# How the masked decays of the second attention are put together in DRAM: accumulating transfers, or plain copies with a skewed write of the mask

## The chip, the cores and the metric

One core of one Trainium2 chip runs the whole program in one launch. The metric is the device time of that launch in microseconds (us). For the kernel before, three timed runs gave 971.83, 976.06 and 982.13 us, so the median is 976.06.

## The reference

The program is a two-layer decoder trunk on 256 tokens of width 1024, all in float32. Layer one holds a differential attention, layer two a "forgetting" attention; each attention sits between two SwiGLU feed-forward blocks, with RMS norms and shifts, scales and gates from a conditioning vector. What the change touches is the logits of the second attention, with 16 heads of width 64:

```python
log_f = jax.nn.log_sigmoid((h @ fgate_w + fgate_b))
F = jnp.cumsum(log_f, axis=1)                     # (b, 256, 16)
...
decay = F[q] - F[k]                               # per head
logits = q @ k.T * scale + decay
logits = jnp.where(q_pos >= k_pos, logits, -inf)
p = softmax(logits)
```

The term F[q] is the same for a whole row, so the softmax does not see it; the kernel adds only -F[k], scaled by 8 because the scores are scaled by 1/8 afterwards, and a large negative constant (-1e30) above the diagonal.

## The kernel before, in words

Every large product is done in three passes: a weight arrives as float32 (`raw`, six buffers of 128 x 1024), ScalarE (ACT) casts its high part (`wh`, six buffers), VectorE (DVE) subtracts to get the low part (`wl`, five buffers), and TensorE (PE) multiplies high by high, low by high and high by low. A tile of such a weight is called a piece here. SyncE (SP) issues the loads of `raw` and of `ada`, the 1 MB blocks of conditioning weights that DVE multiplies and sums in its spare time (the custom operation `ada<-ada,cact,vecs`). The order on PE, ACT, DVE and SP is written out by the program itself (class `InOrder`, L54 to L100, keeps a clock per engine and fills gaps with casts and subtractions; L99 is the one line that records every such instruction). GpSimd (POOL) is called directly as `nc.gpsimd`; its instructions are put in order by the scheduler of the tile framework, and its DMAs go through the software queue q0. The loads by SP go through q1. Both queues use the same 16 DMA engines.

The second attention needs, for each head, a 128 x 384 tile `d` of decays: columns 0 to 127 belong to the first block of 128 queries (keys 0 to 127), columns 128 to 383 to the second block (keys 0 to 255). Each of the two has one 128 x 128 diagonal block, in which the upper triangle must carry the constant.

* While the last value projection of the shared keys and values runs (L1196 to L1228), `fk` (16 heads x 256, minus 8 F[k]) is made at step 7 (L1206 to L1211). POOL stores it twice in DRAM as `fdram`, 384 numbers a head (L1214, L1215). Sixteen DMAs (L1219) then copy each head's 384 numbers to 128 rows of `dmask`, and sixteen more (L1222) add the 128 x 128 mask, which lies in SBUF in the tile `tri`, to the two diagonal blocks of each head: an accumulating DMA, `accum_op=ALU.add`.
* Then a feed-forward block runs, `ffn(1, 0, ...)` (L1232): eleven pairs `pg`, `pu`, and eight outputs `po`. It needs none of this.
* `attention_b` (L1234) begins with two query projections `lp` (`late_pairs`, L1255) while `decay(c)` (L1248) loads the tiles `d0` to `d9` from `dmask`, two for each pair of heads `c`. Their buffers are shared with the hidden tiles of the feed-forward block (tags `hidh2` to `hidh7`, `hidl6` to `hidl9`, list `DT`), so a load waits for the last reader of its buffer. For each pair, `scores` makes the products `sb`, `exps` (L1272) adds the decay with the row minimum on DVE and takes the exponential on ACT, `scale` (L1286) divides, and `weights_t` (L1296) transposes the six 128 x 128 blocks on PE; `values` multiplies by the values. Four projections `lq` and the steps of the output projection `pw` fill PE between these groups.

Of the kernel before, what the change touches and what calls it, by code (L numbers as in the profile page):

```python
# [10 lines left out]
F32 = mybir.dt.float32  # L11
F32R = mybir.dt.float32r
BF16 = mybir.dt.bfloat16
AF = mybir.ActivationFunctionType
ALU = mybir.AluOpType
PSUM = bass.MemoryType.PSUM

P = 128
D = 1024
S = 256  # L20
# [3 lines left out]
BH = 16  # L24
# [5 lines left out]
BIG = 3.0e38  # L30
# [13 lines left out]
NRAW = 6  # L44
NLO = 5
NHI = 6

V_NORM = 0
V_KVN = 48
# [54 lines left out]
def trunk(ctx, tc, a, out):  # L104
    nc = tc.nc
    InOrder.ready = {}
    pe = InOrder(tc, nc.tensor, 0.0, 1 / 2350)
    act = InOrder(tc, nc.scalar, 0.13, 1 / 1200)
    dve = InOrder(tc, nc.vector, 0.08, 1 / 960)
# [14 lines left out]
    def abank(name):  # L124
        return pp.tile([P, 512], F32, tag="ta", name=name)
# [786 lines left out]
    for k in range(0, NC, 2):  # L912
# [3 lines left out]
        if k % 4:  # L916
            i = k // 4
# [14 lines left out]
    def constants():  # L932
# [44 lines left out]
    ident, mask, ub, skew, nlam, subg = (  # L977
        late[n] for n in ("ident", "mask", "ub", "skew", "nlam", "subg"))
# [217 lines left out]
    for i, (kk, n) in enumerate(v_proj("wkv", vb)):  # L1196
        if mh:
            mh.go()
        run_laters()
        if i == 5:  # L1200
            plf = abank("plf")
            for t in range(2):
                pe.transpose(plf[:, t * BH:(t + 1) * BH], lf[:, t * P:(t + 1) * P], ident[:BH, :BH])
            lft = kp.tile([P, 2 * BH], F32, tag="lft", name="lft", bufs=1)
            act.copy(lft, plf[:, :2 * BH])
        if i == 7:  # L1206
            pFk = abank("pFk")
            mm(pFk[:BH, P:S], lft[:, BH:], ub[:, :P], start=True, stop=False, skip_group_check=True)
            mm(pFk[:BH, :S], lft[:, :BH], ub, start=False, stop=True, skip_group_check=True)
            fk = kp.tile([BH, S], F32, tag="w512b", name="fk")  # L1210
            act.activation(fk, pFk[:BH, :S], AF.Copy, scale=-1.0)  # L1211

            fdram = tc.dram_tile([BH, P + S], F32, name="fdram")
            nc.gpsimd.dma_start(fdram[:, :P], fk[:, :P])  # L1214
            nc.gpsimd.dma_start(fdram[:, P:], fk)  # L1215
            dmask = tc.dram_tile([BH, P, 384], F32, name="dmask")
            m2 = mask.rearrange("p (o k) -> p o k", o=1).to_broadcast([P, 2, P])
            for hd in range(BH):
                nc.gpsimd.dma_start(dmask[hd], bass.AP(fdram.tensor, fdram.offset + hd * (P + S), [[0, P], [1, P + S]]))  # L1219
            for hd in range(BH):  # L1220
                diag = dmask[hd].rearrange("p (b k) -> p b k", k=P)[:, ::2]
                nc.gpsimd.dma_start(diag, m2, accum_op=ALU.add)  # L1222
        if i == 8:
            need(*nm_)
            table(AF.Silu)
            mh = MakeH(rstd, nm_)
            mh.go()
# [6 lines left out]
    def attention_b():  # L1234
        o = {}

        def o_tiles(j):
            h = cp_.tile([P, 512], F32R, tag=f"hidh{j}", name=f"obh{j}")
            l = cp_.tile([P, 512], F32R, tag=f"hidl{4 + j}", name=f"obl{j}")
            for i in range(2):  # L1240
                o[2 * j + i] = h[:, i * 256:i * 256 + 256], l[:, i * 256:i * 256 + 256]

        q = [cp_.tile([P, 512], F32, tag=f"hidl{j}", name=f"q{j}") for j in range(4)]
        ds, sms = {}, {}

        DT = ["hidh4", "hidh5", "hidh6", "hidh7", "hidl8", "hidl9", "hidh2", "hidh3", "hidl6", "hidl7"]

        def decay(c):  # L1248

            for hd in (2 * c, 2 * c + 1):  # L1250
                d = cp_.tile([P, 384], F32, tag=DT[hd % 10], name=f"d{hd}")
                nc.gpsimd.dma_start(d, dmask[hd])
                ds[hd] = d

        r = late_pairs("wq", q[:2], None, AF.Exp)  # L1255
        for c in range(5):
            decay(c)
        op = OutProj(o)
        st = {}
        mode[0] = "fill"  # L1260
        NP = BH // 2

        def scores(c, sb):

            cb = (c % 2) * 256
            for qt, (c0, w) in enumerate(QT):
                for m in range(2):
                    rows = slice(m * HD, m * HD + HD)
                    mm(sb[m][:, c0:c0 + w], q[c // 2][rows, cb + qt * P:cb + qt * P + P],
                       kT[c // 2][rows, cb:cb + w], start=True, stop=True)  # L1270

        def exps(c, sb):  # L1272
            nm = kp.tile([P, 4], F32, tag="nm", name=f"nmb{c}")
            sm = kp.tile([P, 4], F32, tag="smb", name=f"smb{c}", bufs=3)
            for m in range(2):
                d = ds[2 * c + m]
                for qt, (c0, w) in enumerate(QT):
                    cc = 2 * qt + m
                    dve.tensor_tensor_reduce(
                        d[:, c0:c0 + w], sb[m][:, c0:c0 + w], d[:, c0:c0 + w], -0.125, BIG,  # L1280
                        ALU.add, ALU.min, accum_out=nm[:, cc:cc + 1])
                    act.activation(d[:, c0:c0 + w], d[:, c0:c0 + w], AF.Exp,
                                   bias=nm[:, cc:cc + 1], scale=-1.0, accum_out=sm[:, cc:cc + 1])
            sms[c] = sm

        def scale(c):  # L1286

            rs = kp.tile([P, 4], F32, tag="rs", name=f"rsb{c}")
            dve.reciprocal(rs, sms[c])
            for m in range(2):  # L1290
                d = ds[2 * c + m]
                for qt, (c0, w) in enumerate(QT):
                    dve.tensor_scalar(d[:, c0:c0 + w], d[:, c0:c0 + w], rs[:, 2 * qt + m:2 * qt + m + 1], None,
                                      op0=ALU.mult)

        def weights_t(c, ta, tb):  # L1296
            for m, b, to, i in ((0, 0, ta, 0), (0, 1, ta, 1), (0, 2, ta, 2), (1, 2, ta, 3), (1, 0, tb, 0), (1, 1, tb, 1)):
                pe.transpose(to[:, i * P:i * P + P], ds[2 * c + m][:, b * P:b * P + P], ident)

        def weights_out(c, ta, tb):  # L1300
            w0 = cp_.tile([P, 512], F32, tag="hidh8", name=f"wta{c}")
            w1 = cp_.tile([P, 256], F32, tag="hidh9", name=f"wtb{c}")
            act.copy(w0, ta)
            dve.tensor_copy(w1, tb[:, :256])
            st[c] = ((w0[:, :2 * P], w0[:, 2 * P:3 * P]), (w1, w0[:, 3 * P:]))

        def values(c, po):

            for kt in range(2):
                for m in range(2):  # L1310
                    hd = 2 * c + m
                    v = vb[kt][hd // 8][:, (hd % 8) * HD:(hd % 8) * HD + HD]
                    mm(po[m * HD:m * HD + HD, kt * P:], v, st[c][m][kt], start=kt == 0, stop=kt == 1)

        def out_split(c, po):
            if c % 2 == 0:
                o_tiles(c // 2)
            oh, ol = o[c]
            act.copy(oh, po)
            dve.tensor_tensor(ol, po, oh.bitcast(F32), op=ALU.subtract)  # L1320

        def group(t):

            cs, cw, cv = (c if 0 <= c < NP else None for c in (t, t - 1, t - 2))
            sb = [sbank(f"sb{t}_{m}") for m in range(2)] if cs is not None else None
            ta = abank(f"wa{t}") if cw is not None else None
            tb = bbank(f"wb{t}") if cw is not None or cv is not None else None
            if cs is not None:
                scores(cs, sb)
            if cv is not None:  # L1330
                values(cv, tb[:, 256:])
            if cw is not None:
                weights_t(cw, ta, tb)
            if cs is not None:
                plain(exps, cs, sb)
            if cw is not None:
                weights_out(cw, ta, tb)
            if cv is not None:
                out_split(cv, tb[:, 256:])
            if cw is not None and t + 4 < NP:  # L1340
                decay(t + 4)

        def fills():
            for j in (2, 3):
                for _ in late_pair("wq", q[j], r, f"lq{j}"):
                    yield
                    yield
            for _ in range(6):
                for _ in op.steps():
                    yield  # L1350

        fill = fills()
        for t, n in enumerate((3, 9, 7, 7, 8, 8, 7, 7, 7, 5)):
            for i in range(n):
                if 1 <= t <= NP and i == n - 2:
                    scale(t - 1)
                next(fill)
            group(t)
        for _ in range(4):
            next(fill)  # L1360
        return op, fill
# [135 lines left out]
```

## Time and profile before

| what | value |
|---|---|
| timed runs | 971.83, 976.06, 982.13 us |
| the profiled execution, its own time | 971.96 us |
| its span in the trace | 970.1 us |
| granted TensorE clock | 0.998 |
| busy: PE, PE weight load, DVE, ACT, POOL | 959.5, 933.0, 819.2, 551.0, 81.8 us |
| DMA queue q1 (SP's loads) | 259.69 MB |
| DMA queue q0 (POOL's transfers) | 12.16 MB |

The profiled execution is one run, 1.86 us longer than its span, and 4.1 us below the median of the timed ones. Matmuls overlap one another in the pipeline: a matmul of 128 x 256 shows 276 ns, and six of them take 0.68 us on the chain of waits. In the rows of a view, "a<-b" names the tile written and the tiles read, and "DMA landing" is the time from the issue of a transfer to its last byte. The queue rows give packets, megabytes and the time that their packets took as a share of 16 DMA engines over the window asked for.

### The profile page before, as it was taken

The numbers are of one execution on the slowest core, as the hardware profiler recorded it, in microseconds if no ns is written. First come the engines' busy times: TensorE is split into PE (matmuls) and PEld (weight loads), VectorE is DVE, ScalarE is ACT, GpSimd is POOL, SyncE is SP. The second block draws the span as 40 slices with busy tenths as digits, with TensorE's granted clock in tenths as the row PEclk, the third lists the DMA queues.
The fourth block names the chain that finished last, engine by engine and source line by source line (L and its number), as shares of the span: only waits on it lengthen the run. The fifth ranks groups of instructions, "written<-read, shape, count | busy, mean of one in ns | idle before, by whom it ended". The sixth has DMA issues, their size and how long they took to land.

```text
span 970.1 us, 20433 instructions
## 1 busy us (share of the span) xinstructions
PE 959.5 (99%) x8076; PEld 933.0 (96%) x8076; DVE 819.2 (84%) x1372; ACT 551.0 (57%) x894; POOL 81.8 (8%) x126
## 2 busy tenths in 40 slices
PE   8999999999999999999999999999999999999997
PEld 7999999998999999999998999999998899999997
DVE  7989979889999999888889988899978799555575
ACT  5466545566787745545577544545567776555432
POOL 0000200000112000000000720000021014300000
PEclk9999999999999999999999999999999999999999
DMA  9998899967867699888959999998884337987641
GB/s 359 414 359 277 324 377 343 338 227 266 309 202 257 199 373 379 315 267 317 329 190 373 343 357 359 399 369 326 321 321 161 109 110 232 269 156 268 188 150 44
DMA packets 74849, 273.46 MB, mean 282 GB/s; under 512 B 9929, under 2 KB 14833, under 8 KB 64642
## 3 DMA queue, kind: packets, MB, share of 16 engines
q1 hardware_dynamic: 66016, 259.69, 75.3%
q0 software_dynamic: 8448, 12.16, 5.0%
q8 instruction: 63, 1.03, 0.4%
q10 hardware_dynamic: 290, 0.32, 0.1%
q14 instruction: 32, 0.26, 0.1%
HBM read 267.90 MB, written 7.90 MB: 284 GB/s over the span
## 4 chain that ended last, share of the span: by engine, by line
PE 96%; DVE 2%; DMA 1%; ACT 1%; issue 0%; SPq 0%; ACTq 0%; DVEq 0%
PE po L99 25%; PE pg L99 21%; PE pu L99 21%; PE pf L99 5%; PE pv L99 5%; PE pw L99 4%; PE lp L99 4%; PE pqk L99 3%; PE lq L99 1%; PE lg L99 1%; PE lu L99 1%; PE pk L99 1%; DVE ada L99 1%; DMA ada<-in_ada 1%; PE sb L99 1%; PE s L99 1%
## 5 line engine op out<-in xcount | busy, mean ns | idle before, releaser
L99 ACT CAST wh<-raw 128x1024 fp32r<-128x1024 f32 (+1 forms) x360 | 347.2, 975 | 222.8 <-PE po L99 68.2
L99 DVE TENSOR_TENSOR wl<-raw,wh 128x1024 fp32r<-128x1024 f32 (+1 forms) x360 | 398.2, 1125 | 69.3 <-ACT sg L99 17.6
L99 DVE CUSTOM_DVE_ANT_0 ada<-ada,cact,vecs 128x1024 f32<-128x1024 f32 x160 | 203.4, 1278 | 0.4 <-DMA ada<-in_ada 0.4
L99 PE MATMUL pg<-HH,wl 128*128 128x256 f32 x608 | 168.2, 277 | 0.4 <-DVE wl L99 0.4
L99 PE MATMUL pg<-HH,wh 128*128 128x256 f32 x608 | 168.0, 276 | 0.0
L99 PE MATMUL pg<-HL,wh 128*128 128x256 f32 x608 | 167.9, 276 | 0.0
L99 PE MATMUL pu<-HH,wh 128*128 128x256 f32 x608 | 167.9, 276 | 0.0
L99 PE MATMUL pu<-HL,wh 128*128 128x256 f32 x608 | 167.9, 276 | 0.0
L99 PE MATMUL pu<-HH,wl 128*128 128x256 f32 x608 | 167.9, 276 | 0.0
L99 PE MATMUL po<-hidh,wh 128*128 128x256 f32 x528 | 145.7, 276 | 0.0
L99 PE MATMUL po<-hidh,wl 128*128 128x256 f32 x528 | 145.7, 276 | 0.0
L99 PE MATMUL po<-hidl,wh 128*128 128x256 f32 x528 | 145.7, 276 | 0.0
L99 PEld LDWEIGHTS pg<-HH,wl 128*128 128x128 f32 x608 | 114.2, 188 | 0.9 <-DVE wl L99 0.8
L99 PEld LDWEIGHTS pg<-HH,wh 128*128 128x128 f32 x608 | 114.1, 188 | 0.7 <-ACT tri L99 0.6
L99 PEld LDWEIGHTS pg<-HL,wh 128*128 128x128 f32 x608 | 114.2, 188 | 0.0
L99 PEld LDWEIGHTS pu<-HH,wh 128*128 128x128 f32 x608 | 114.2, 188 | 0.0
L99 PEld LDWEIGHTS pu<-HH,wl 128*128 128x128 f32 x608 | 114.2, 188 | 0.0
L99 PEld LDWEIGHTS pu<-HL,wh 128*128 128x128 f32 x608 | 114.1, 188 | 0.0
L99 PEld LDWEIGHTS po<-hidh,wl 128*128 128x128 f32 x528 | 99.1, 188 | 0.0
L99 PEld LDWEIGHTS po<-hidh,wh 128*128 128x128 f32 x528 | 99.1, 188 | 0.0
L99 PEld LDWEIGHTS po<-hidl,wh 128*128 128x128 f32 x528 | 99.1, 188 | 0.0
L99 DVE TENSOR_TENSOR hidl<-hf,hidh 128x512 fp32r<-128x512 f32 x44 | 30.3, 689 | 21.7 <-ACT hidh L99 21.7
(225 smaller groups left out, 1860.9 us busy)
## 6 DMA issues: line engine op xcount, KB each, us to landing
raw<-in_win SPq DMA_DIRECT2D x176, 512.0 KB, 7.7
ada<-in_ada SPq DMA_DIRECT2D x79, 1024.0 KB, 7.7
raw<-in_wout SPq DMA_DIRECT2D x48, 384.0 KB, 5.7
raw<-in_wout SPq DMA_DIRECT2D x48, 320.0 KB, 5.4
raw<-in_wqk SPq DMA_DIRECT2D x16, 512.0 KB, 5.6
raw<-in_wo SPq DMA_DIRECT2D x16, 512.0 KB, 5.5
raw<-in_wlast SPq DMA_DIRECT2D x16, 512.0 KB, 4.3
raw<-in_wv SPq DMA_DIRECT2D x8, 512.0 KB, 6.5
```

The costliest lines, as they stand in the source:

```text
L99: return self.tc.keep_in_program_order(f(*args, **kw))
```

## The change

`fdram` holds each head once (256 numbers). The DRAM tensor is now called `masked` and has 512 columns a row (`DW`) instead of 384. For each of its two parts, columns 0 to 255 (the second query block) and then columns 256 to 383 (the first), four DMAs of four heads each copy `fdram` to all rows, and four DMAs of four heads each write the constant over the upper triangle. The triangle is written as 127 runs of 127 numbers (508 bytes) with a pitch of 513: each run begins one column further right than the one before. What a run writes beyond its block falls into the columns of the next part, which is copied afterwards, or into columns that nobody reads. The source of the runs is one row of the mask in the input `in_misc`, read again and again. In `d` the two parts have changed places, so `exps`, `scale` and `weights_t` address them through `DQ`; every instruction keeps its shape and its turn.

```diff
-            fdram = tc.dram_tile([BH, P + S], F32, name="fdram")
-            nc.gpsimd.dma_start(fdram[:, :P], fk[:, :P])
-            nc.gpsimd.dma_start(fdram[:, P:], fk)
-            dmask = tc.dram_tile([BH, P, 384], F32, name="dmask")
-            m2 = mask.rearrange("p (o k) -> p o k", o=1).to_broadcast([P, 2, P])
-            for hd in range(BH):
-                nc.gpsimd.dma_start(dmask[hd], bass.AP(fdram.tensor, fdram.offset + hd * (P + S), [[0, P], [1, P + S]]))
-            for hd in range(BH):
-                diag = dmask[hd].rearrange("p (b k) -> p b k", k=P)[:, ::2]
-                nc.gpsimd.dma_start(diag, m2, accum_op=ALU.add)
+            fdram = tc.dram_tile([BH, S], F32, name="fdram")
+            nc.gpsimd.dma_start(fdram, fk)
+            masked = tc.dram_tile([BH, P, DW], F32, name="masked")
+            for c0, w in ((0, S), (S, P)):
+                for hd in range(0, BH, 4):
+                    nc.gpsimd.dma_start(masked[hd:hd + 4, :, c0:c0 + w],
+                                        bass.AP(fdram.tensor, fdram.offset + hd * S, [[S, 4], [0, P], [1, w]]))
+                for hd in range(0, BH, 4):
+                    above = bass.AP(masked.tensor, masked.offset + hd * P * DW + c0 + w - P + 1,
+                                    [[P * DW, 4], [DW + 1, P - 1], [1, P - 1]])
+                    nc.gpsimd.dma_start(above, bass.AP(a["misc"].tensor, a["misc"].offset + 2 * P + 1,
+                                                       [[0, 4], [0, P - 1], [1, P - 1]]))
...
+        DQ = (S, 0)
...
-                nc.gpsimd.dma_start(d, dmask[hd])
+                nc.gpsimd.dma_start(d, masked[hd, :, :384])
...
+                    dq = d[:, DQ[qt]:DQ[qt] + w]
                     dve.tensor_tensor_reduce(
-                        d[:, c0:c0 + w], sb[m][:, c0:c0 + w], d[:, c0:c0 + w], -0.125, BIG,
+                        dq, sb[m][:, c0:c0 + w], dq, -0.125, BIG,
                         ALU.add, ALU.min, accum_out=nm[:, cc:cc + 1])
...
-            for m, b, to, i in ((0, 0, ta, 0), (0, 1, ta, 1), (0, 2, ta, 2), (1, 2, ta, 3), (1, 0, tb, 0), (1, 1, tb, 1)):
+            for m, b, to, i in ((0, 2, ta, 0), (0, 0, ta, 1), (0, 1, ta, 2), (1, 1, ta, 3), (1, 2, tb, 0), (1, 0, tb, 1)):
```

On PE, DVE, ACT and SP the list of instructions is the same before and after, in the same order and shapes (7858, 1268, 674 and 261 rows). Only POOL's list differs, in two places. The first is the building of the decays in DRAM, during the value projection and the feed-forward block after it. Before (`fg` is a small weight loaded ahead of it, `x16` means sixteen of the same kind in a row):

```order
L1165 DMA fg<-in_fgw 128x128
L1214 DMA fdram<-fk 16x128
L1215 DMA fdram<-fk 16x256
L1219 DMA dmask<-fdram 128x384 x16
L1222 DMA dmask<-tri 128x2x128 x16
L1252 DMA d_9428<-dmask 128x384
```

Now, with the semaphores that each transfer waits for (DMASW0 to DMASW7 are completion semaphores of POOL's transfers, used in turn):

```order
L1216 DMA fdram<-fk 16x256 [waits Activation_49]
L1220 DMA masked<-fdram 512x1x256 [waits DMASW2_49]
L1220 DMA masked<-fdram 512x1x256 x3
L1225 DMA masked<-in_misc 4x127x127 [waits DMASW7_49,DMASW3_49]
...
L1225 DMA masked<-in_misc 4x127x127 [waits DMASW6_49]
L1220 DMA masked<-fdram 512x1x128 [waits DMASW7_49]
...
L1220 DMA masked<-fdram 512x1x128 [waits DMASW2_49]
L1225 DMA masked<-in_misc 4x127x127 [waits DMASW3_49]
...
L1225 DMA masked<-in_misc 4x127x127 [waits DMASW6_49]
```

Thirty-four transfers have become seventeen, in four steps of four: within a group of four heads, copy, constant, copy and constant each wait for the one before to land, and the four groups overlap.

The second place is the loading of the first ten tiles `d0` to `d9` on POOL, at the end of the feed-forward block. Before:

```order
L1252 DMA d6_9428<-dmask_6811 128x384 [waits DMASW4_49,DVE_49,PE_49]
L1252 DMA d7_9430<-dmask_6811 128x384 [waits DMASW5_49,DVE_49,PE_49]
L1252 DMA d0_9416<-dmask_6811 128x384 [waits DMASW6_49,DVE_49,PE_49]
L1252 DMA d1_9418<-dmask_6811 128x384 [waits DMASW7_49,PE_49]
L1252 DMA d2_9420<-dmask_6811 128x384 [waits DMASW0_49,DVE_49,PE_49]
L1252 DMA d8_9432<-dmask_6811 128x384 [waits DMASW1_49,PE_49]
...
L1252 DMA d5_9426<-dmask_6811 128x384 [waits DMASW4_49,DVE_49,PE_49]
L1252 DMA d9_9434<-dmask_6811 128x384 [waits DMASW5_49]
```

Now:

```order
L1258 DMA d0_9399<-masked_6810 128x384 [waits DMASW7_49,DVE_49,PE_49]
L1258 DMA d1_9401<-masked_6810 128x384 [waits PE_49]
L1258 DMA d2_9403<-masked_6810 128x384 [waits DVE_49,PE_49]
L1258 DMA d3_9405<-masked_6810 128x384 [waits DVE_49,PE_49]
L1258 DMA d4_9407<-masked_6810 128x384 [waits DMASW0_49,DVE_49,PE_49]
L1258 DMA d5_9409<-masked_6810 128x384 [waits DVE_49,PE_49]
...
L1258 DMA d8_9415<-masked_6810 128x384 [waits DMASW3_49]
L1258 DMA d9_9417<-masked_6810 128x384 [waits DMASW4_49]
```

The loads now come in the order of the heads; before, `d6` and `d7`, whose buffers come free first, stood at the front.

More of the change, by code (lines that the diff above doesn't have):

```diff
@@ L46 @@
 NHI = 6
+DW = 512
 V_NORM = 0
@@ L1278, in exps @@
                     cc = 2 * qt + m
+                    dq = d[:, DQ[qt]:DQ[qt] + w]
                     dve.tensor_tensor_reduce(
-                        d[:, c0:c0 + w], sb[m][:, c0:c0 + w], d[:, c0:c0 + w], -0.125, BIG,
+                        dq, sb[m][:, c0:c0 + w], dq, -0.125, BIG,
                         ALU.add, ALU.min, accum_out=nm[:, cc:cc + 1])
-                    act.activation(d[:, c0:c0 + w], d[:, c0:c0 + w], AF.Exp,
+                    act.activation(dq, dq, AF.Exp,
                                    bias=nm[:, cc:cc + 1], scale=-1.0, accum_out=sm[:, cc:cc + 1])
@@ L1292, in scale @@
                 for qt, (c0, w) in enumerate(QT):
-                    dve.tensor_scalar(d[:, c0:c0 + w], d[:, c0:c0 + w], rs[:, 2 * qt + m:2 * qt + m + 1], None,
+                    dq = d[:, DQ[qt]:DQ[qt] + w]
+                    dve.tensor_scalar(dq, dq, rs[:, 2 * qt + m:2 * qt + m + 1], None,
                                       op0=ALU.mult)
         def weights_t(c, ta, tb):
-            for m, b, to, i in ((0, 0, ta, 0), (0, 1, ta, 1), (0, 2, ta, 2), (1, 2, ta, 3), (1, 0, tb, 0), (1, 1, tb, 1)):
+            for m, b, to, i in ((0, 2, ta, 0), (0, 0, ta, 1), (0, 1, ta, 2), (1, 1, ta, 3), (1, 2, tb, 0), (1, 0, tb, 1)):
                 pe.transpose(to[:, i * P:i * P + P], ds[2 * c + m][:, b * P:b * P + P], ident)
```

## The prediction

> **What bounds the kernel now.** I read the page's head first, then the waits of PE, then the stretches around the change. The head:
>
> ```profile
> span 970.1 us, 20433 instructions
> PE 959.5 (99%) x8076; PEld 933.0 (96%) x8076; DVE 819.2 (84%) x1372; ACT 551.0 (57%) x894; POOL 81.8 (8%) x126
> PE 96%; DVE 2%; DMA 1%; ACT 1%; issue 0%; SPq 0%; ACTq 0%; DVEq 0%
> ```
>
> TensorE is busy 959.5 of 970.1 us and holds 96% of the chain that ended last. Whatever is done elsewhere, at most 970.1 - 959.5 = 10.6 us could go, and the start and the last store lie in that. PE's waits over the whole run:
>
> ```profile
> PE pf L99 <- ACT HH L99: 1.9, 1, 1.9
> PE warm L99 <- DVE one L99: 1.2, 1, 1.2
> PE pg L99 <- DVE wl L99: 0.4, 1, 0.4
> PE wa L99 <- DVE d L99: 0.2, 1, 0.2
> ```
>
> (Columns: total us, times, longest.) None names a transfer of POOL. The nearest is `wa` on `d`, 0.2 us: the transposes of the last heads wait for the division, not for a load. Now the stretches in which the decays are built and read; the columns after PE are its weight load, DVE, ACT, POOL, then the granted clock, the DMA engines' share and GB/s:
>
> ```profile
> 531.00:547.00 16.00, 16.00 (x120) 15.09 (x119) 15.30 (x26) 9.80 (x14) 11.53 (x20) 1.00 0.94 316
> 547.00:575.00 28.00, 28.00 (x250) 28.00 (x249) 24.34 (x32) 13.28 (x16) 12.53 (x11) 1.00 1.10 360
> 575.00:600.00 25.00, 25.00 (x223) 25.00 (x222) 21.34 (x29) 10.68 (x13) 3.58 (x3) 1.00 1.11 358
> 620.00:640.00 20.00, 20.00 (x179) 20.00 (x178) 18.62 (x25) 11.40 (x14) 0.00 (x0) 1.00 1.02 413
> 660.00:680.00 20.00, 20.00 (x179) 20.00 (x178) 18.57 (x31) 9.91 (x16) 0.00 (x0) 1.00 0.87 322
> ```
>
> PE is full in every one at a clock of 1.00, while the DMA engines are saturated (0.94 to 1.11) until after 620 us and come down to 0.87 by 660 us. So the building does load the DMA engines; the load shows as waits on ACT, which does not bound anything here:
>
> ```profile
> ACT wh L99 <- DMA raw<-in_win: 35.1, 22, 3.6
> POOL dmask L1222 <- DMA dmask<-tri: 21.0, 8, 3.2
> ```
>
> Between that and PE stand the converted pieces. How far ahead they are is seen where the piece changes width:
>
> ```profile
> 646.40 0.95 DVE L99 TENSOR_TENSOR wl<-raw,wh 128x768 fp32r<-128x768 f32 x1
> 655.88 0.28 PE L99 MATMUL po<-hidh,wl 128*128 128x256 f32 x1
> ```
>
> The first piece of the output weights is finished at 646.40 + 0.95 = 647.35 us and first used at 655.88: a lead of 8.5 us. That is what weights may be late before PE notices.
>
> **The change part by part.** First the building, as POOL and the two queues show it:
>
> ```profile
> 525.63 0.52 POOL L1214 DMA_DIRECT2D fdram<-fk  x1 [33.69 <-ACT fk L99]
> 532.38 4.16 POOL L1219 DMA_DIRECT2D dmask<-fdram  x8 [5.75 <-DMA fdram<-fk]
> 583.62 1.20 POOL L1222 DMA_DIRECT2D dmask<-tri  x1 [2.59 <-DMA dmask<-tri]
> 710.52 4.83 POOL L1252 DMA_DIRECT2D d<-dmask  x8 [125.71 <-PE po L99]
> 716.35 1.06 POOL L1252 DMA_DIRECT2D d<-dmask  x2 [0.99 <-DVE x L99]
> ```
>
> POOL issues the last addition at 583.62 and then has nothing to do until a buffer comes free at 710.52.
>
> *POOL's time.* The rows by line:
>
> ```profile
> L1219 POOL DMA_DIRECT2D dmask<-fdram x16: 523/523/544, 532.4 to 543.1; - x16
> L1222 POOL DMA_DIRECT2D dmask<-tri x16: 1182/1197/1855, 543.6 to 583.6; - x16
> DMA to landing us min/median/max: 12.3/30.2/32.1
> ```
>
> The first takes 523 ns for 128 runs, the second 1197 ns for 256. A copy of 512 runs is then 4 x 0.523 = 2.1 us and a constant of 508 runs 2 x 1.197 = 2.4 us; eight of each make 36 us against 16 x 0.52 + 16 x 1.2 = 27.5 us. Nobody waits for POOL there: 0.
>
> *DMA engine time*, what really could reach PE. In two windows, one nearly pure in copies, one in additions:
>
> ```profile
> q0 software_dynamic: 856, 2.67, 50.4%
> q1 hardware_dynamic: 638, 2.38, 43.8%
> dmask<-fdram POOLq DMA_DIRECT2D x16, 192.0 KB, 6.6
> ...
> q1 hardware_dynamic: 1754, 8.06, 83.8%
> q0 software_dynamic: 1755, 0.85, 26.8%
> ```
>
> From 531 to 547 us q0 takes 0.504 x 16 us x 16 engines = 129 engine-us for 2.67 MB, 48 a megabyte. From 575 to 600 it takes 0.268 x 25 x 16 = 107 engine-us for 1755 packets, 61 ns each, at 512 bytes. Before: copies 3.15 MB x 48 = 151, additions 16 x 256 = 4096 x 61 ns = 250, in all 401 engine-us, 25 us of each engine. After: the copies move the same 3.15 MB in 4096 runs, so 151 (by bytes) to 250 (if each run cost as much as an addition); the constants are 8 x 508 = 4064 runs of 508 bytes, 2.06 MB, so 99 (by bytes) to 248 (as an addition). I take 151 for the copies, nearest to the old ones in source and bytes, and 248 for the constants, whose size is that of the additions though nothing is added: 399, no change. The ends are 250 and 498: 9.4 us less or 6.1 us more on each engine.
>
> On the constants, row and rule can be set side by side. The Trainium skill ("DMA: Bandwidth & Descriptors", section Specifications) says that a transfer needs 512 bytes or more for line rate and that below this the engine reads, modifies and writes. By it the 508-byte runs cost like the additions, and the sum would stay near 399 engine-us rather than fall to 250; no row of this run has a 508-byte write.
>
> What that does to PE: more engine time is late weights, and 6.1 us is less than the lead of 8.5 us, with spare room (share 0.87) from 660 us on. Less engine time makes weights earlier, and PE waits for none in these stretches. Both ends give 0. If the lead were gone, each further us would cost 1 us.
>
> *The order of landing.* The chain is now fdram, copy, constant, copy, constant, each waiting on POOL for the one before of its group, with the next groups queued behind it there, and behind them the loads of `d`. It starts at 525.63 and POOL's first copy at about 532. A copy of 512 KB landed like a weight piece of 512 KB, a constant like an addition or twice that:
>
> ```profile
> raw<-in_win SPq DMA_DIRECT2D x38, 512.0 KB, 12.3
> dmask<-tri POOLq DMA_DIRECT2D x16, 128.0 KB, 30.2
> ```
>
> Four issues of 2.1 us put the last group's first copy at 540; then 12.3 + 60 + 12.3 + 60 = 145 us at worst is 685, and 12 + 10 + 12 + 10 at best 584 us. The loads are not due before 710.52: 25 us of cover at the worst, so 0.
>
> *The loads of `d`.* Same number, same bytes; a row of 1536 bytes now ends every 2048. Before, they landed quickly, and were first needed late:
>
> ```profile
> d<-dmask POOLq DMA_DIRECT2D x16, 192.0 KB, 5.2
> L99 DVE CUSTOM_DVE_ANT_0 d<-sb,d x32: 285/356/422, 730.1 to 764.3; 128x128 f32<-128x128 f32 x16, 128x256 f32<-128x256 f32 x16
> ```
>
> In the new order `d0` leads and its buffer `hidh4` is read 4 matmul steps of `po` after `hidh2`, 4 x 3 x 0.113 = 1.4 us later (six matmuls take 0.68 us). Loads thus begin about 712 instead of 710.52 and end about 717.4 as now; `d0` is in SBUF near 717, 13 us before 730.1. If that cover were gone, DVE's first `exps` would be late by the difference. Cost 0.
>
> *The new places in `d`.* The same instructions on other columns: 0.
>
> Sum against the profiled execution's own time (971.96, 1.86 above its span): 971.96 + 0 + 0 + 0 = 972. The timed runs before have their median 4.1 us higher, at 976.06, and nothing in the trace says on which side of it a new set will fall; I put the forecast between the two, 974.0.
>
> **The rivals.**
>
> *Four engines instead of sixteen (slower).* The outermost dimension of every new transfer is four heads; before, it was 128 partitions. If a transfer is spread over engines by that dimension and always from the first on, the 399 engine-us fall on four engines, 100 us each instead of 25. At q0's share of 50.4% beside the weights this takes 198 us, at 26.8% 373 us. From 532 it ends between 730 and 905, later than the loads are due; `d0` then lands 5 us after, at 735 at the earliest, 5 us after the 730.1 of the first `exps`: 977. And weights on those engines would by then be late by more than the lead: q1 got 0.84 of the engines from 575 to 600 us, so at 0.50 it falls (0.84 - 0.50) x 198 = 67 us behind, less 8.5 = 59 us of stall: 1031. I put it between, at 1000. It decides once the chain passes 710.52 or the lead is used up. Against it: four such transfers are in flight at once, and if each takes the next four engines, the sixteen share the load as before.
>
> A sentence on this from the Trainium skill ("DMA: Bandwidth & Descriptors", Rules for kernel authors, with the section on why a DMA increments its semaphore by 16): an outermost dimension of four does confine a DMA to four engines, and on POOL's path these are taken in turn from a cursor. By that rule the load is even, and this rival fails; no transfer of POOL's in this trace has fewer than eight rows outermost, so nothing here shows it.
>
> *Dear runs (slower).* If a 508-byte run that begins at odd places cost three times an addition, 183 ns, the constants take 744 engine-us, and the whole 895, 31 us more on each engine. Off that go 8.5 us of lead and (1 - 0.87) x 70 us = 9 us of spare until the attention: 13 us of stall, 985. For it speaks only that no such run is in the trace; against it, that an addition of the same size, which reads its target too, takes 61 ns.
>
> *The load falls and the timed runs gain (faster, a little).* If the constants go by bytes, the building takes 9.4 us less of each engine. The profiled execution shows nothing to gain, but the timed runs spread over 10 us; if that spread were weights that arrive too late around 531 to 620 us, the median would fall to the lowest, 972, and with 0.2 us of `wa` and 0.4 of `wl` to 971. A gain of over 1% (9.8 us) has no place to come from: it would need nearly all of the 10.6 us in which PE is idle, which lie at the start and the end.
>
> **How the numbers follow.** No change 0.76, the small gain 0.10, four engines 0.07, dear runs 0.07. A measurement of this kernel tells about 1% from no change. Faster by over 1% gets 0.03, since only a lucky set of runs could show it; slower gets the two slow rivals less their milder forms, 0.12; the rest, 0.85, is the same. The range reaches down to 968 (the profiled time less what a lucky set gives, 4 us) and up to 984, the highest timed run and 2 us; beyond it lie the larger part of the slow rivals.
>
> **What would show it.** Right: PE stays full at 1.00 from 531 to 640 us with no wait on `wl`, q0's packets between 531 and 620 us sum to 250 to 500 engine-us, the last constant is issued before 690 us, loads of `d` begin near 712 and the first `exps` near 730. Wrong: a wait of `pg`, `pu` or `po` on `wl` in the feed-forward block, `exps` waiting for `d`, or a POOL that is still building after 710 us.

## The result, and the profile after

The change makes the kernel slower. Its timed runs gave 1018.01, 1021.88, 1021.97 and 1025.02 us, median 1021.92, against 973.94 (971.77 to 982.13, four runs) for the kernel before: a ratio of 1.0474, with a 95% interval of 1.0401 to 1.0548. The forecast was 974.0, with a range up to 984.

The profiled execution after took 1025.02 us. The head of its page, answering to the head of before:

```profile
span 1023.2 us, 20415 instructions
PE 975.6 (95%) x8076; PEld 946.1 (92%) x8076; DVE 819.3 (80%) x1372; ACT 550.1 (54%) x894; POOL 71.6 (7%) x109
PE 86%; DMA 8%; DVE 3%; ACT 1%; issue 0%; POOL 0%; DVEq 0%; ACTq 0%
```

The span grew by 1023.2 - 970.1 = 53.1 us. PE is busy 16.1 us longer with the same 8076 matmuls, and 8% of the chain that ended last is now DMA, where it was 1%. PE's waits between 500 and 900 us (total, times, longest):

```profile
PE pg L101 <- ACT wh L101: 27.8, 3, 16.9
PE pg L101 <- DVE wl L101: 8.8, 7, 2.4
PE wa L101 <- DVE d L101: 0.2, 1, 0.2
```

These are waits for weight pieces in the feed-forward block; `wa` on `d`, where the decays are used, has the 0.2 us that it had before. Over the whole run the two weight waits are 27.8 and 9.3 us, 36.7 more than the 0.4 of before. So 36.7 + 16.1 = 52.8 of the 53.1 us are accounted for. The stretches after, whose columns are those of the prediction (PE, weight load, DVE, ACT, POOL, granted clock, DMA share, GB/s):

```profile
531.00:547.00 16.00, 16.00 (x117) 15.01 (x116) 15.27 (x25) 9.59 (x14) 6.56 (x6) 1.00 0.94 305
547.00:575.00 28.00, 25.77 (x210) 25.37 (x210) 13.80 (x19) 7.04 (x9) 3.48 (x4) 0.94 1.03 196
575.00:600.00 25.00, 12.76 (x82) 12.07 (x82) 9.24 (x13) 5.04 (x6) 4.38 (x4) 0.73 0.92 208
600.00:620.00 20.00, 17.80 (x154) 17.41 (x154) 15.61 (x22) 6.75 (x8) 3.42 (x3) 1.00 1.03 232
620.00:640.00 20.00, 3.05 (x23) 2.55 (x22) 0.66 (x1) 1.25 (x2) 0.00 (x0) 0.63 0.96 117
640.00:660.00 20.00, 16.94 (x109) 16.74 (x110) 13.93 (x20) 8.76 (x11) 0.00 (x0) 0.77 0.96 324
660.00:680.00 20.00, 20.00 (x172) 20.00 (x171) 18.63 (x25) 10.15 (x13) 0.00 (x0) 1.00 0.98 361
```

Two things are to be seen. The DMA engines are as busy as before (0.92 to 1.03), but they move 117 to 232 GB/s from 547 to 640 us in place of the 358 to 413 of before. And where PE stalls, its granted clock falls, to 0.73, 0.63 and 0.77: from 575 to 600 us the 82 matmuls take 12.76 us, 156 ns each, where a full stretch of before has 25.00 / 223 = 112 ns. The two queues from 530 to 700 us, first before, then after:

```profile
q1 hardware_dynamic: 13267, 54.64, 84.3%
q0 software_dynamic: 5405, 5.26, 15.3%
```

```profile
q1 hardware_dynamic: 8566, 38.37, 62.8%
q0 software_dynamic: 5277, 5.32, 33.9%
```

POOL's queue moves the same bytes (5.26 and 5.32 MB) and takes 33.9 - 15.3 = 18.6% more of 16 engines over 170 us, which is 31.6 us on each engine. What that does to the weights is seen in SP's loads from 530 to 640 us (count, then the landings), before and after:

```profile
L99 SPq DMA_DIRECT2D raw<-in_win x37: 327/328/328, 529.8 to 631.7; - x37
...
DMA to landing us min/median/max: 4.5/12.0/14.1
```

```profile
L101 SPq DMA_DIRECT2D raw<-in_win x22: 327/1184/5947, 530.4 to 632.8; - x22
...
DMA to landing us min/median/max: 7.2/24.2/40.6
```

Twenty-two pieces are loaded in place of 37, and one takes up to 40.6 us to land in place of 14.1. Counted from the trace's packet records, the constants are 448 packets of 4572 bytes (nine runs of 508) with a mean of 1635 ns, 182 ns a run, and 733 engine-us in all (the times of all packets added up, over the 16 engines); the large packets of the copies, 768 of 4096 bytes, take 134.

The building itself ends in time. POOL's instructions (start, duration):

```profile
531.65 4.38 POOL L1220 DMA_DIRECT2D masked<-fdram  x4 [4.96 <-DMA fdram<-fk]
...
588.45 1.10 POOL L1220 DMA_DIRECT2D masked<-fdram  x1 [18.52 <-DMA masked<-in_misc]
...
611.86 1.14 POOL L1225 DMA_DIRECT2D masked<-in_misc  x1 [2.92 <-DMA masked<-fdram]
764.83 1.93 POOL L1258 DMA_DIRECT2D d<-masked  x3 [151.83 <-PE po L101]
```

The last constant is issued at 611.86, and the loads of `d` start at 764.83, when PE frees their buffers, not when the constants are done. The time is lost in the feed-forward block, to late weights, and not in the attention that the change serves.

### The profile page after: what moved, and what is told of

The parts are those of the page before. It is cut to its first block, busy times and chain, and to the rows that moved or that the text cites. A ratio compares the mean times of both kernels' runs of the same rounds, so it can differ in the third digit from the quotient of the medians.

```text
span 1023.2 us, 20415 instructions
## 1 busy us (share of the span) xinstructions
PE 975.6 (95%) x8076; PEld 946.1 (92%) x8076; DVE 819.3 (80%) x1372; ACT 550.1 (54%) x894; POOL 71.6 (7%) x109
## 3 DMA queue, kind: packets, MB, share of 16 engines
q8 instruction: 63, 1.03, 0.4%
## 4 chain that ended last, share of the span: by engine, by line
PE 86%; DMA 8%; DVE 3%; ACT 1%; issue 0%; POOL 0%; DVEq 0%; ACTq 0%
PE po L101 24%; PE pg L101 18%; PE pu L101 17%; DMA raw<-in_win 7%; PE pf L101 5%; PE pv L101 4%; PE lp L101 3%; PE pqk L101 3%; PE pw L101 3%; DMA ada<-in_ada 1%; DVE ada L101 1%; DVE wl L101 1%; PE lq L101 1%; PE lu L101 1%; PE lg L101 1%; PE pk L101 1%
## 5 line engine op out<-in xcount | busy, mean ns | idle before, releaser
L101 PE MATMUL pg<-HH,wh 128*128 128x256 f32 x608 | 171.3, 282 | 27.8 <-ACT wh L101 27.8
L101 PE MATMUL pg<-HH,wl 128*128 128x256 f32 x608 | 171.6, 282 | 9.3 <-DVE wl L101 9.3
L101 PE MATMUL pg<-HL,wh 128*128 128x256 f32 x608 | 170.4, 280 | 0.0
L101 PE MATMUL pu<-HL,wh 128*128 128x256 f32 x608 | 170.0, 280 | 0.0
L101 PE MATMUL pu<-HH,wh 128*128 128x256 f32 x608 | 170.0, 280 | 0.0
L101 PE MATMUL pu<-HH,wl 128*128 128x256 f32 x608 | 170.0, 280 | 0.0
L101 PEld LDWEIGHTS pg<-HH,wh 128*128 128x128 f32 x608 | 116.5, 192 | 29.1 <-ACT wh L101 29.1
L101 PEld LDWEIGHTS pg<-HH,wl 128*128 128x128 f32 x608 | 116.8, 192 | 11.3 <-DVE wl L101 11.3
L101 PEld LDWEIGHTS pg<-HL,wh 128*128 128x128 f32 x608 | 116.4, 191 | 0.0
```

What stands on the lines that cost most here:

```text
L101: return self.tc.keep_in_program_order(f(*args, **kw))
```

## The experiments

The first theory was that runs of 508 bytes at odd places are dear by themselves, as the second rival had it. Others were that the four heads outermost confine a transfer to few engines, that the copies are at fault, and that all runs read one and the same row of DRAM. Short diffs are against the kernel after; "before" in brackets is the kernel before on the same chip. A time without an interval is that of one run; packets are counted from the trace's records.

**e1, the copies alone.**

```diff
-                for hd in range(0, BH, 4):
-                    above = bass.AP(masked.tensor, ...)
-                    nc.gpsimd.dma_start(above, ...)
```

> The constants are left out, so the decays carry no mask; the eight copies of four heads each stay. If the constants alone cost the time, TensorE waits for no weight between 531 and 660 us and the time is 972 (970 to 977). If the copies, which also have four heads outermost, share in it, the time stays above 985. The copies' 151 to 250 engine-us of the prediction should show as 9 to 16 us of each engine.

Measured: 972.83 us [971.82]. PE's largest wait for a weight piece in it, and q0 from 530 to 700 us:

```profile
PE pg L101 <- DVE wl L101: 0.5, 1, 0.5
```

```profile
q0 software_dynamic: 3232, 3.21, 6.1%
```

The 6.1% are 10.4 us of each engine, within the 9 to 16 that were expected. The copies, their landings and the new layout cost nothing that one run can show. The loss belongs to the constants.

**e2, e3, e4: length and place of the run.** e2 writes aligned runs of 512 bytes, e3 aligned runs of 508 bytes, e4 skewed runs of 512.

```diff
# e2
+                    above = bass.AP(masked.tensor, masked.offset + hd * P * DW + c0 + w - P,
+                                    [[P * DW, 4], [DW, P - 1], [1, P]])
# e3: as e2, with runs [1, P - 1]
# e4: as after, with runs [1, P]
```

> The constants become 127 runs of 512 bytes that all begin at the same aligned column, a rectangle instead of a triangle, so the mask is wrong. Short-run theory (below 512 bytes a write is dear) and odd-start theory (a run is dear because it begins at a shifting odd address): a run falls from 184 ns to 30 to 60 ns, 972 to 976. One-source theory (all runs read the same bytes) and four-engine theory (four heads outermost confine each transfer to four engines): nothing changes, 1015 to 1025.

> As the run before with 508 instead of 512 bytes, aligned start, a rectangle, so the mask is wrong. Short-run theory: dear as in the changed kernel, 1015 to 1025. Odd-start theory: cheap, 972 to 976. One-source and four-engine theory: 1015 to 1025.

> The triangle with its pitch of 513 as in the change, but each run has 128 numbers, 512 bytes; the last number falls where nothing reads it, so the computation is whole. Short-run theory: cheap, 972 to 976. Odd-start theory: dear, 1015 to 1025. One-source and four-engine theory: 1015 to 1025.

Measured: 1014.94, 1023.49 and 1018.01 us [971.82]. A run takes 134, 150 and 184 ns. PE's waits in e2, which has neither a short run nor an odd place:

```profile
PE pg L101 <- ACT wh L101: 13.5, 3, 9.3
PE pg L101 <- DVE wl L101: 9.4, 10, 2.2
```

The constants stay dear in it, and it is still 43 us above before. The theory of dear runs in that form falls: the skew adds 32 ns a run at 508 bytes and 50 at 512, but 134 are there without it.

**e5, e6: other source rows.** In e5 each of the 127 runs of a head reads its own row of the input `in_misc` (at a place where every row holds the constant), in e6 each head has a row of its own, which its 127 runs read. The order stays, four heads outermost.

```diff
# e5
-   bass.AP(a["misc"].tensor, a["misc"].offset + 2 * P + 1, [[0, 4], [0, P - 1], [1, P - 1]])
+   bass.AP(a["misc"].tensor, a["misc"].offset + 1279, [[0, 4], [1670, P - 1], [1, P - 1]])
# e6
+   bass.AP(a["misc"].tensor, a["misc"].offset + 1279 + 1670 * hd, [[1670, 4], [0, P - 1], [1, P - 1]])
```

> The change as it is, but each of a constant's 127 runs reads its own row of the input instead of all reading one row; the computation is whole. One-source theory (every run of all sixteen engines reads the same 508 bytes of DRAM, and these reads queue up): a run falls from 182 ns to 30 to 90 ns, 972 to 985; the engines may walk the rows in step, so part of the price may stay. Four-engine theory (four heads outermost confine each transfer to four engines): 1015 to 1025.

> The change as it is, but each head's runs read a row of their own, sixteen rows in all, each read 127 times by one transfer, as the copies read fdram; the computation is whole. One-source theory: a run falls from 182 ns to about the copies' price, 30 to 60 ns, 972 to 978. If reading one row again and again is dear in itself: 1015 to 1025, and then the many rows alone are cheap. Four-engine theory: 1015 to 1025.

Measured: 989.49 and 988.84 us [975.75]. The same packets of nine runs now take 245 and 253 ns instead of 1635. So one row that all transfers read is what makes them dear: the destinations, sizes and order are those of after. A row read by one head's 127 runs costs hardly more than a row for each run. Both times lie above the ranges that were expected: 13 to 14 us of the loss are left.

**e7, the rows outermost.** One source row as in after, but 128 rows outermost and the four heads inside.

```diff
-                                    [[P * DW, 4], [DW + 1, P - 1], [1, P - 1]])
+                                    [[DW + 1, P], [P * DW, 4], [1, P - 1]])
...
-                                                       [[0, 4], [0, P - 1], [1, P - 1]]))
+                                                       [[0, P], [0, 4], [1, P - 1]]))
```

> The constants with 128 rows as the outermost dimension and the four heads inside it, one row read by all as in the change; the computation is whole. Four-engine theory: each transfer spreads over sixteen engines, the weights are served evenly, 972 to 985. One-source theory: the price of a run stays near 180 ns, 1010 to 1025.

Measured: 1030.19 us [975.75], 1872 ns a packet. Its waits:

```profile
PE pg L101 <- ACT wh L101: 37.0, 4, 17.5
PE pg L101 <- DVE wl L101: 6.8, 6, 3.2
```

The outermost dimension is not the cause: with 128 it is no better.

**e8 and e15: the additions of before in the new layout.** The copies of four heads stay; the constant is added from SBUF, head by head, to both diagonal blocks.

```diff
+            for hd in range(BH):
+                nc.gpsimd.dma_start(masked[hd, :, P:P + S].rearrange("p (b k) -> p b k", k=P), m2, accum_op=ALU.add)
```

> The copies and the layout of the change, with the constant added from SBUF by sixteen accumulating transfers as before; the computation is whole. All theories that put the cost in how the constants are written: 970 to 977, additions near 61 ns each. If the layout, the order of the d tiles or the copies cost anything: above 980.

> e8 again (the new layout and the new copies, the constant added from SBUF as before), measured in rounds. If the remainder belongs to the constants and not to the copies of four heads or to the new layout of the loads, 970 to 979 us with a ratio whose interval holds 1.000. If the copies or the layout carry part of it, 979 to 986 us.

Measured: e8 975.70 us [975.75]; e15 973.44 (972.17 to 979.68, ten runs) against 973.41 (nineteen), ratio 1.0003, with a 95% interval of 0.9975 to 1.0032. An addition's packet of 512 bytes takes 64 ns. All of the loss is the way the constant is written.

**e9 and e12: the remainder.** e9 is e7 with a source row for each run; e12 is e5 again, with four runs.

```diff
# e9, against e7
-   bass.AP(a["misc"].tensor, a["misc"].offset + 2 * P + 1, [[0, P], [0, 4], [1, P - 1]])
+   bass.AP(a["misc"].tensor, a["misc"].offset + 1279, [[1670, P], [0, 4], [1, P - 1]])
```

> Each run reads its own row, and the constants have 128 rows outermost instead of four heads; the computation is whole. If the rest of the loss (a wait of 8.4 us of TensorE for weights with four heads outermost, weights that land after 20 us instead of 13) is the confinement of a transfer to four engines: no wait over 1 us, weights land in 10 to 14 us, 970 to 980. If it has another cause (the runs' size, the four steps one after another): waits of 4 to 10 us as with four heads outermost, 980 to 992.

> The kernel with a source row for each run and four heads outermost, timed in rounds beside its twin with rows outermost. If four heads outermost cost something of their own: 5 to 15 us more than the twin, beyond the interval. If not: the two agree.

Measured: e9 985.18 us (ratio 1.0112, 1.0065 to 1.0160), e12 984.72 (1.0112, 1.0040 to 1.0185), against 974.06. With four heads or 128 rows outermost no difference in time is seen. About 37 of the 48 us are gone, 11 are left, though q0 now takes less engine time than before the change (10.9% in e12, 15.3% before).

**e10 and e11: is it the place of the row, or the number of its readers?** In e10 the one row lies in a DRAM tensor of the program's own. In e11 each transfer has its row, shared by its four heads.

```diff
# e10
+            cdram = tc.dram_tile([1, P], F32, name="cdram")
+            nc.gpsimd.dma_start(cdram, a["misc"][:1, 2 * P + 1:3 * P + 1])
...
+   bass.AP(cdram.tensor, cdram.offset, [[0, 4], [0, P - 1], [1, P - 1]])
# e11
+   bass.AP(a["misc"].tensor, a["misc"].offset + 1279 + 1670 * hd, [[0, 4], [0, P - 1], [1, P - 1]])
```

> All runs read one row, as in the change, but a copy of it in a DRAM tensor of the program's own instead of the input tensor; the computation is whole. One-source theory: dear as in the change, about 180 ns a run, 1010 to 1030. If it is where the input tensor lies that makes it dear: 25 to 30 ns a run, 975 to 992.

> Four rows in all, one for each transfer and so shared by four heads; the computation is whole. One-source theory with a row served at one run in 20 ns whoever asks: a packet of nine runs takes about 0.2 us with one reader and 0.5 to 0.7 us with the three or four that share it, between the 0.25 of a row for each head and the 1.64 of one row for all; 985 to 1000. If one row read by four is as dear as by sixteen: 1015 to 1025; if sharing does not matter below sixteen: 972 to 990, 0.25 us.

Measured: e10 1023.65 us and 1484 ns a packet, e11 1002.10 us and 651 ns. It is not the input's place. The price follows the number of readers of a row. q0 from 530 to 700 us, in e11 and then in e12:

```profile
q0 software_dynamic: 5280, 5.33, 17.9%
```

```profile
q0 software_dynamic: 5260, 5.31, 10.9%
```

| readers of a row | ns a packet of nine runs | us [before on the same chip] |
|---|---|---|
| after: all transfers | 1635 | 1021.92 [973.94] |
| e11: the four heads of a transfer | 651 | 1002.10 [974.06] |
| e6: one head | 253 | 988.84 [975.75] |
| e12: one run of a head (four heads share it) | 242 | 984.72 [974.06] |

The same is seen inside the kernel after, when its packets of nine runs are sorted by how many packets of constants were in flight, in the mean, beside and with each: below 2 a packet takes 0.19 us (median, of seven packets only), with 2 to 4 it takes 0.61, with 4 to 6 1.12, with 8 to 10 1.88 and with 10 to 12 2.05 us. In e9 it is 0.19 to 0.20 in each of these classes. So runs that read one row stand in line for it: in after, eleven packets of nine runs in 2.05 us make one run every 21 ns (17 to 26 in the other classes above 2). Whether it is these bytes that are served one run at a time, or a larger piece of the memory around them, no run here tells.

**e13 and e14: where the last 11 us are.** e13 writes runs of 512 bytes at multiples of 512; e14 takes the constant from SBUF.

```diff
# e13, against e9
+   above = bass.AP(masked.tensor, masked.offset + hd * P * DW + c0 + w - P, [[DW, P], [P * DW, 4], [1, P]])
+   bass.AP(a["misc"].tensor, a["misc"].offset + 1278, [[1670, P], [0, 4], [1, P]])
# e14, against e9
+            neg = cp_.tile([P, P], F32, tag="hidh10", name="neg")
+            nc.gpsimd.memset(neg, NEG)
...
+   nc.gpsimd.dma_start(above, neg[:, :P - 1].rearrange("p (o k) -> p o k", o=1).to_broadcast([P, 4, P - 1]))
```

> As e9 (each run its own source row, 128 rows outermost), but the runs are 512 bytes long and start at multiples of 512 bytes: the constant then lies over a rectangle and not over the triangle. If the remaining 11 us come from runs that begin at odd places, 970 to 978 us and no wait of PE on weights of over 1 us. If they come from reading the constants in DRAM, or from packets of eight or nine runs, 980 to 992 us with 3 to 8 us of waits on the weight pieces, as in e9 and e12.

> As e9, but the runs of the constant come from a tile in SBUF, one partition for each row of the decays, filled once by POOL; the whole computation. Still plain writes with the skewed pitch. If the remaining 11 us come from reading the constants in DRAM, 970 to 978 us and no wait of PE on weights of over 1 us. If they come from the odd starts, or from the form of the packets (if these stay long), 980 to 992 us. If one packet is now a single run of 508 bytes, as the additions were, and the form is the cause, 970 to 978 us too; then the size of a packet in the trace tells the two apart from e13.

Measured: e13 975.93 us (1.0008, 0.9981 to 1.0034), e14 986.38 (1.0145, 1.0107 to 1.0183), against 973.41. The packets are long in both (eight runs in e13, nine and five in e14), so their form does not cost, nor does the reading from DRAM: e14 reads none of its constants there. How the written runs lie does. Where the read runs begin shows no price: counted from the start of `in_misc`, one in eight of e13's sources begins at a multiple of 64 bytes, the others at other multiples of 8, and e13 is level with before.

**e16, e17, e18: length, odd start, and which start.**

```diff
# e16: as e13, with runs [1, P - 1]
# e17, against e13
-   [[DW, P], [P * DW, 4], [1, P]]   from c0 + w - P
+   [[DW + 1, P], [P * DW, 4], [1, P]]   from c0 + w - P + 1
# e18, against e13
-   [[DW, P], [P * DW, 4], [1, P]]
+   [[DW - 16, P], [P * DW, 4], [1, P]]
```

> As e13, but each run is 508 bytes long, still starting at a multiple of 512 bytes: the constant lies over a rectangle less its last column. If the length under 512 bytes is what costs, 982 to 990 us, packets of over 1 us among the constants and weights that land after 15 us or more. If it is the odd start, 971 to 979 us, as e13 (975.9).

> As e9, but each run is 512 bytes long, on the skewed pitch: every run starts at another odd place (the whole computation; the 128th number falls where e9's neighbours are rewritten or not read). If the odd start costs, 982 to 990 us with 3 to 8 us of waits of PE on weight pieces. If the length costs, 971 to 979 us.

> As e17, but with a pitch of 496 numbers, so that runs of 512 bytes start at multiples of 64 bytes, nearly none of them a multiple of 512 (the constant then lies over other places than the triangle). If a start at a multiple of 64 bytes is enough, 971 to 979 us; if it must be a multiple of 512 bytes, 982 to 990 us as e9. If e17 is level with before, this one is too.

Measured, against 972.10: e16 976.27 us (1.0021, 0.9991 to 1.0051), e17 987.68 (1.0115, 1.0049 to 1.0180), e18 971.89 (0.9992, 0.9966 to 1.0019). In e17 a run's source begins one number early, so the first place above the diagonal does not hold the constant; its shapes and bytes are those described. The length of 508 bytes cannot be told from no cost; starts that step through all multiples of 4 bytes (the odd starts) cost 1.1%; starts at multiples of 64 bytes cost nothing that these runs can show. SP's queue from 575 to 610 us in e17, e18 and before:

```profile
q1 hardware_dynamic: 1978, 9.11, 82.3%
```

```profile
q1 hardware_dynamic: 2566, 11.87, 88.0%
```

```profile
q1 hardware_dynamic: 2395, 11.35, 84.1%
```

A megabyte of SP's queue, mostly weights, takes 0.823 x 35 x 16 / 9.11 = 50.6 engine-us beside odd writes, and 41.5 in e18 and before. By the same count the other runs with odd starts have 46.6 (e12), 47.0 (e9) and 47.6 (e14), the other two without them 40.7 (e13) and 43.3 (e16). So the odd writes slow the reads of the other queue, and PE feels it. Why they do, no run here shows. The stretches of e17, then of e18:

```profile
547.00:575.00 28.00, 26.98 (x238) 26.78 (x237) 18.77 (x26) 8.62 (x11) 6.68 (x7) 1.00 1.02 321
575.00:600.00 25.00, 20.54 (x158) 20.05 (x157) 13.99 (x17) 7.67 (x9) 2.25 (x3) 0.86 1.02 296
600.00:620.00 20.00, 18.20 (x140) 17.80 (x139) 18.00 (x25) 11.00 (x13) 0.00 (x0) 0.91 0.96 350
```

```profile
547.00:575.00 28.00, 28.00 (x250) 28.00 (x249) 25.19 (x34) 13.57 (x16) 6.73 (x8) 1.00 1.02 394
575.00:600.00 25.00, 25.00 (x223) 25.00 (x222) 17.98 (x24) 10.11 (x12) 2.25 (x3) 1.00 1.02 395
600.00:620.00 20.00, 20.00 (x179) 20.00 (x179) 18.62 (x25) 10.08 (x13) 0.00 (x0) 1.00 0.97 351
```

At the same DMA share (1.02) e18 moves 394 GB/s and PE never stops; e17 moves 321 and 296, PE misses 1.0 + 4.5 + 1.8 = 7.3 us, and its clock falls to 0.86. This run of e17 is its slowest, 18 us above the 972.10 of before: 8.7 us of its matmuls ran at half the clock, an estimated 4.4 us lost, and the rest fits the slower pace of PE that the last section shows.

None of the variants is faster than the kernel before. Of those that do the whole computation only the one with the additions of before is level with it (e8, e15).

## Why the prediction was wrong, point by point

**The step that failed is the price of the constants**, "248 (as an addition)", with its bounds of 99 and 248. It measured 733 engine-us. The upper bound was no bound: it took the nearest row, the addition of 512 bytes at 61 ns, as the most that a run of that size could cost. What set the new transfers apart was neither size nor place but their source, which the section on the change even names: one row of `in_misc`, read 4064 times. With rows of their own, 4032 of the 4064 runs take 108 (e12, packets of 4572 bytes), close to the lower bound of 99.

The copies of before read one row of `fdram` by 128 descriptors too, and took 48 us a megabyte. There, sixteen heads had sixteen rows; e6, with one row for each head, is cheap as well. The trace of before thus held no case of one row for everything, and the prediction did not ask for the effect of the 0s in the source.

**A second term was put at nothing:** that the constants change the price of SP's own packets. The prediction counted only the engine time of q0. In e12 q0 takes less of it than before, 10.9% against 15.3%, so by that sum nothing should be lost; 11 us are, by the odd starts of the writes. Of the 48 us, 37 thus go with the one source row and 11 with the odd starts.

**Runs below 512 bytes.** The Trainium skill ("DMA: Bandwidth & Descriptors", Specifications) has a read-modify-write below 512 bytes. What runs below that cost is little here: e16's runs of 508 bytes measured 1.0021 (0.9991 to 1.0051), and a packet of nine such runs takes 189 ns in the median and 218 in the mean, 21 and 24 ns a run, beside 21 and an estimated 21 for the 512-byte runs of e13 (165 ns for eight in the median; for the mean, 133 engine-us for the copies, which have the same size, are taken off). With one source row the step is 134 to 150 ns a run (e2, e3). What costs more is a start at odd places. The Trainium skill ("DMA: Bandwidth & Descriptors", How a descriptor splits into AXI transactions) makes reads that do not start at a multiple of 256 bytes dearer. For these writes the boundary is lower: three of four starts in e18 miss the 256 bytes, and it is level with before.

**"The lead of 8.5 us ... with spare room" failed with it.** The dear-runs rival had the price nearly right, 744 engine-us and 31 us more on each engine; measured are 733 and 31.6. It is not the odd place that made it, and its time, 985, was 37 us short. It took 8.5 us of lead and 9 us of spare room off the 31. The spare room lies after 660 us, when PE had already stood still, and a stall of the engine that bounds the kernel is not repaid. The 36.7 us of waits are even more than 31.6. SP's own packets became dearer too: 0.628 x 170 x 16 / 38.37 = 44.5 us a megabyte after, 42.0 before, which is an estimated 6 us more on each engine.

The lead itself was mis-sized. The 8.5 us were read at one piece, the first of the output weights. Counted over the 44 input pieces of the block, from the end of a piece's subtraction to the first matmul that reads `wl`, the lead of before is 4.3 to 10.8 us, least for the piece used at 615 us; the 6.1 us of the prediction's own upper end were already more than that. In after the piece used at 564 us still has 8.7 us, and the next one, at 569, 0.1. In e12 the lead is used up by 594 us. In e15, with the additions of before, the least is 0.3 us: level with before, but with little to spare.

**"Each further us would cost 1 us" was too little.** PE lost 36.7 us waiting and was busy 16.1 us longer for the same matmuls. By the trace's clock records the granted clock was 0.5 for 41.0 us between 570 and 657 us; PE worked in 18.9 of them, so an estimated 9.4 of the 16.1 us belong to the clock. The Trainium skill ("TensorE: Matmul & The Clock Gate", Why this matters for your kernels) states that an idle gap of a few us brings the clock down to half. The trace agrees in kind: means of 0.63 to 0.77 in the slices with long stalls. The other 6.7 us fit the slower pace from 660 us on, 172 matmuls in 20 us where before had 179; that pace also comes without stalls (last section), so its part may be chance.

**What held.** POOL's time cost nothing (1.1 us for each transfer; 2.1 and 2.4 were forecast). The copies are 134 engine-us in their large packets, 151 forecast for all, and e1 shows no loss. The last packet of the constants ends at 647 us, within the 584 to 685 forecast for the chain. The loads of `d` begin at 764.83 and the first `exps` at 783.2 us; less the 53.1 us of the span that is 711.7 and 730.1, as forecast (712 and 730). The four-engines rival fails, as argued: e9 and e12 show no difference between 128 and four outermost. The prediction took every new transfer to have four outermost; in the list of instructions only the constants stand with four (`4x127x127`), and the copies with 512 (`512x1x256`). Of the signs of being wrong that the prediction named, the first one came: `pg` waits for `wl`.

## What to carry to other kernels

A step of 0 over a DRAM source is not free because the bytes are few: here one row read by all transfers at once raised a packet from a mean of 0.24 to 1.64 us, and a row for each head was enough to be rid of it. Transfers off the critical path still set the length of that path when they share DMA engines with weights whose stream is saturated, so price a new transfer by what it does to the other queue, source and destination apart. Let written runs start at multiples of 64 bytes, the smallest step that was tried and free; a skew by one number took 1.1 to 1.5% here (e9, e12, e14, e17).

## What the runs showed of the hardware that was not expected

* One DRAM row served about one run of 508 bytes every 21 ns, however many read it. It makes little difference whether the row lies in an input or in the program's own tensor (182 and 165 ns a run).
* Slow packets of one queue starve the other. From 557 to 567 us, when the packets of constants in q0 took 1.95 us in the median, the share of SP's queue fell to 30.8%, where the additions of before had left it 83.0%. First before, then after:

```profile
q1 hardware_dynamic: 716, 3.18, 83.0%
q0 software_dynamic: 717, 0.34, 27.3%
```

```profile
q0 software_dynamic: 160, 0.28, 71.0%
q1 hardware_dynamic: 206, 0.96, 30.8%
```

  The Trainium skill ("DMA: Bandwidth & Descriptors", Queues, rings and completion order) has the engines take turns between queues packet by packet. The trace agrees: before, the two queues had 716 and 717 packets served in these 10 us. After, a weight's packet takes 0.18 us and a constant's 1.95 (medians); in turn, they leave the weights a small part of the time.
* Writes at odd starts slowed the reads of another queue (46.6 to 50.6 us a megabyte in e9, e12, e14 and e17, 40.7 to 43.3 in e13, e16, e18 and before). Their own median hardly moves (192 ns for nine runs in e9, 189 in e16), their mean does (328 against 218).
* PE showed two steady paces at a granted clock of 1.00. This stretch of the kernel after, long past the last stall, has 172 matmuls where before had 179:

```profile
700.00:720.00 20.00, 20.00 (x172) 20.00 (x171) 18.28 (x29) 10.34 (x15) 0.00 (x0) 1.00 0.90 320
```

  It comes and goes for 40 to 200 us, also without stalls: by the spacing of the matmuls' starts, from 320 to 520 us in e2 and e16, far ahead of the change, and from 800 to 920 us in e18. At 7 matmuls in 20 us, 200 us of it cost 8 us, about the spread of the runs before. What sets it no run here shows.
